# Moving the products of old states between the transposes of their own head, in an mLSTM layer streamed through TensorE

## The chip, the cores and the metric

The kernel runs on one core of one Trainium2 chip. The metric is the device time of one execution in microseconds (us); the median of the runs of one kernel is compared with the median of another.

## What is computed

The reference is one inference step of a two-layer decoder trunk, with the same weights for a prompt group (1 sequence of 256 tokens) and a sample group (8 sequences of 8 new tokens with a state from earlier steps), all in float32. Layer 0 mixes tokens by a chunked spatial gate, layer 1 by an mLSTM with 8 heads; each is followed by a gated MLP with a causal width-3 convolution. The change touches only the mLSTM of layer 1. Cut to what matters, one head's chunk of that layer computes:

```python
sc  = einsum('td,sd->ts', q, k) * w_intra               # scores inside the chunk
num = w_inter * einsum('td,de->te', q, C) + einsum('ts,se->te', sc, v)
den = w_inter * einsum('td,d->t', q, n) + sum(sc)
h   = num / max(abs(den), exp(-m_t))                    # then normed, gated by o, times w_out
C_new = decay * C + einsum('sd,se->de', k * g, v)       # the new state, an output
n_new = decay * n + sum(k * g)
```

`q`, `k` (128 wide) and `v`, `o` (256 wide) of each head come out of one product of the normed input with `b_w_in`. For the sample group `C` and `n` are inputs, one 128 x 256 matrix and one vector for each of 8 sequences and 8 heads; the prompt group starts from zero states, so for it the first term of `num` falls away. The term of the old states, `w_inter * (q C)`, and the new states `C_new` are the two places that the change moves.

## The kernel before, in words

**Blocks.** The 320 token columns (256 of the prompt, 64 of the samples) are kept transposed in SBUF. Weights are streamed once, in blocks of 128 output columns and up to 8 x 128 input rows. A block's raw float32 weights (512 KB) come by a DMA on SyncE's queue, four blocks ahead (`prefetch`, `AHEAD`), are split into a high part `wh` on ScalarE (L173) and a low part `wl` on VectorE (L174), one block ahead, and each 128 x 128 piece is multiplied three times: `wh` with the high and the low part of the input, `wl` with the high part. In the mLSTM layer a block's eight `wl` products stand last (`low_last`). A block is 24 matmuls of 128 x 320 into a PSUM buffer `pm`.

**Order.** TensorE's instructions keep the order in which the program writes them (`pin` in `mm` and `tr`, L69 and L72). The other engines' order is made by the scheduler from the program's order, data and the marks `issue_after`. PSUM is divided in two pools: `psm` with 3 buffers (blocks) and `psa` with 5 (everything else).

**The loop over heads.** `layer_b` computes the gates and the first blocks of head 0 in `gates`, then runs one iteration for each head `h`, in which blocks of head `h` alternate with what is left of head `h - 1`. Iteration `h` issues, in this order:

- `rows_in(h)` (L839): the row of decays of this head, broadcast to 128 partitions by a DMA; two blocks for `q` and `k`, each with its epilogue `qk_epi`
- `inter(h - 1)` (L947 to L955): the products of the old states. 16 matmuls `num<-C,Qz`, 32 columns of `Qz` against one sequence's state `C` (128 x 258, `n` and a padding column included), two per 32-row strip of one PSUM tile. `Qz` holds the scaled sample queries of the head, spread so that each sequence meets its own state, and is written by VectorE in `scores` (L870); for head 0 from the PSUM tile `pMb`, for the others from the row of `rows_in`
- `numer(h - 1)`: `num<-vh,Ps` (two, added to the same tile) and `num` from `vh`, `vl`, `Ph`, `Pl`, the products with `v`
- a `v` block; `stats(h - 1)`; `state_prompt(h - 1)` (`pCp`); `state_sample(h - 1, 0)`; another `v` block
- `state_sample(h - 1, 1)`, `scores(h)` (`psc`, then `w`, `dec` L868, `Qz` L870, `Pf`, `Ph`, `Pl`, `Ps`), an `o` block, `state_sample(h - 1, 2)`
- `state_in(h)` (L944): four DMAs of 258 KB, two sequences' states each, into 8 buffers `C0`; the trace calls the tile `C`
- another `o` block; `finish(h - 1)`: six transposes `phn<-ident,hn` of the normed output
- `state_sample(h - 1, 3)`: as for each pair `i`, two matmuls `pcs<-vb,kgz` or `pcs<-vh,kgz`, two VectorE updates `C<-C,dec,pcs` in place (L1032), and a DMA `out_Cs<-C` (L1033)
- `k_nat(h)`: three transposes `pk<-ident,qs` of the keys, from which ScalarE and VectorE make `kgs` (L919, L920), `kgh` and `kgl`
- `v_nat(h)`: six transposes `pv<-ident,vTb` of the values into two PSUM tiles, from which ScalarE and VectorE make `vh` (L892) and `vl` (L895)

Head 0 has no part of a head before it: in its iteration only `scores`, `k_nat` and `v_nat` stand, behind the blocks in `gates`. Its states are loaded one by one in `gates`. Head 7's iteration is written apart (`last`): `state_in(7)` stands behind its second `v` block, and `finish(6)` and the pairs 2 and 3 come earlier. Between blocks, `early` issues blocks of the output projection over the first eight pieces of the result (`pm<-yhb,wh`). Behind the loop the tail computes two pieces of that projection (`begin(0)`, `begin(1)`, four and two rows deep), then `inter(7)`, `numer(7)` and the rest of head 7.

Of the kernel before, what the change touches and what calls it, by code (L numbers as in the profile page):

```python
# [25 lines left out]
NH = 8  # L26
# [26 lines left out]
class Net:  # L53
# [622 lines left out]
    def layer_b(self):  # L676
        nc, tc, I, O = self.nc, self.tc, self.I, self.O
# [4 lines left out]
        with ExitStack() as ctx:  # L682
# [18 lines left out]
            def pairs(x):  # L701

                return x.rearrange("p (j e) -> p j e", e=16)
# [127 lines left out]
            def v_epi(h, j, ps):  # L831
                vT = lp.tile([P, 384], F32, tag="vT", name="vTb", bufs=2)
                nc.scalar.copy(vT[:, :T], ps[:, :T])
                nc.scalar.copy(vT[:, T:384], ps[:, TP:T])  # L834
                S[h].setdefault("vT", []).append(vT)
# [68 lines left out]
            def k_nat(h):  # L904
                s = S[h]
                ks = s["k"][0]
                pool, tag = (self.psm, "pm") if 0 < h < NH - 1 else (self.psa, "pa")
                pk = pool.tile([P, 512], F32, tag=tag, name="pk")
                for t in range(3):
                    self.tr(pk[:, t * P:(t + 1) * P], ks[:, t * P:(t + 1) * P], self.ident)  # L910
                kgh = hp.tile([P, 2, P], F32R, tag="kgh", name="kgh", bufs=1)
                kgl = hp.tile([P, 2, P], F32R, tag="kgl", name="kgl", bufs=1)
                kgs = hp.tile([P, 2, P], F32R, tag="kgs", name="kgs", bufs=1)
                kgz = hp.tile([P, NB, P], F32R, tag="kgz", name="kgz", bufs=1)
                g = colsT[:, 2, 32 + h:33 + h]
                src = pk[:, 2 * P:3 * P]

                for i, (r, o) in enumerate(((slice(0, 32), slice(32, 64)), (slice(32, 64), slice(0, 32)))):
                    nc.scalar.activation(kgs[:, i, :], src, AF.Copy, scale=g)  # L919
                    nc.vector.scalar_tensor_tensor(kgs[o, i, :], src[r], g[r], kgs[r, i, :].bitcast(F32), op0=MULT, op1=SUB)  # L920
                s["kg"] = (kgh, kgl, kgs, kgz)
                if h < NH - 1:
                    k_mask(h)
                for t in range(2):
                    g = colsT[:, t, 32 + h:33 + h]
                    src = pk[:, t * P:(t + 1) * P]
                    nc.scalar.activation(kgh[:, t, :], src, AF.Copy, scale=g)
                    nc.vector.scalar_tensor_tensor(kgl[:, t, :], src, g, kgh[:, t, :].bitcast(F32), op0=MULT, op1=SUB)
# [11 lines left out]
            def state_in(h):  # L940
                S[h].setdefault("C", [])
                for i in range(4) if h else (len(S[h]["C"]),):
                    C0 = lp.tile([P, 2, CW], F32, tag="C0", name="C0", bufs=8)
                    nc.sync.dma_start(C0, I["C0"][h, :, 2 * i:2 * i + 2, :])  # L944
                    S[h]["C"].append(C0)

            def inter(h):  # L947

                s = S[h]
                s["num2"] = self.psa.tile([P, 512], F32, tag="pa", name="num")  # L950
                for c in range(2):
                    for j in range(4):
                        b = 2 * j + c
                        z = NS + 32 * b - NS * c
                        mm(s["num2"][32 * j:32 * j + 32, :CW], Qz[:, z:z + 32], s["C"][j][:, c, :], c == 0, False, skip=True)  # L955
# [62 lines left out]
            def state_sample(h, i, later=False):  # L1018
                s = S[h]
                kgz, dec, C0 = s["kg"][3], s["P"][2], s["C"][i]  # L1020

                wide = h < NH - 2 or h == NH - 2 and i < 2
                pcs = [pool.tile([P, 512], F32, tag=tag, name="pcs") for pool, tag in
                       ((self.psa, "pa"), (self.psm, "pm") if wide else (self.psa, "pa"))]
                for u in range(2):
                    b = 2 * i + u
                    mm(pcs[u][:, :CW], kgz[:, b, :], vh[:, 2, :] if b < 4 else vb, True, True)

                def update():
                    for u in range(2):  # L1030
                        b = 2 * i + u
                        made = nc.vector.scalar_tensor_tensor(C0[:, u, :], C0[:, u, :], dec[:, b:b + 1], pcs[u][:, :CW], op0=MULT, op1=ADD)  # L1032
                    nc.sync.dma_start(O["Cs"][h, :, 2 * i:2 * i + 2, :], C0)  # L1033
                    return made

                return update if later else update()
# [8 lines left out]
            def finish(h):  # L1045
                s = S[h]
                yh = hp.tile([P, 2, T], F32R, tag="yhb", name="yhb", bufs=6)
                yl = hp.tile([P, 2, T], F32R, tag="ylb", name="ylb", bufs=6)
                for e in range(2):
                    pt = self.psa.tile([P, 512], F32, tag="pa", name="phn")  # L1050
                    for t in range(3):
                        self.tr(pt[:, t * P:(t + 1) * P], hn[:, t, e * P:(e + 1) * P], self.ident)
                    y = self.tp.tile([P, T], F32, tag="yf", name="y_b", bufs=2)
                    o = s["o"][e]
                    nc.vector.scalar_tensor_tensor(y[:, :TP], o[:, :TP], 1.0, pt[:, :TP], op0=ADD, op1=MULT)
                    nc.vector.scalar_tensor_tensor(pairs(y[:, TP:]), pairs(o[:, TP:]), 1.0, apart(pt[:, TP:384]), op0=ADD, op1=MULT)
                    g = gnh[:, 2 * h + e:2 * h + e + 1]
                    yp, h2, l2 = parity(y), halves(yh[:, e, :]), halves(yl[:, e, :])
                    nc.scalar.activation(h2, yp, AF.Copy, scale=g)
                    nc.vector.scalar_tensor_tensor(l2, yp, g, h2.bitcast(F32), op0=MULT, op1=SUB)  # L1060
                    Y[2 * h + e] = (yh[:, e, :], yl[:, e, :])
# [27 lines left out]
            def blk():  # L1089
                return self.block(KD, self.x_rhs)  # L1090
# [12 lines left out]
            for h in range(NH):  # L1103
                if h:
                    rows_in(h)
                    qk_epi(h, 0, blk())
                    early(h, 0)
                    qk_epi(h, 1, blk())
                    inter(h - 1)
                    numer(h - 1)  # L1110
                    early(h, 1)
                    ps = blk()
                    with self.behind_split():
                        stats(h - 1)
                    v_epi(h, 0, ps)
                    state_prompt(h - 1)
                    made = state_sample(h - 1, 0)
                    early(h, 2)
                    v_epi(h, 1, blk())
                last = h == NH - 1  # L1120
                if last:
                    with tc.issue_after(made.ins):
                        normed(h - 1)
                    with tc.issue_after(self.last_load.ins):
                        state_in(h)
                if h == 1:
                    o_epi(h, 0, blk())
                if h:
                    made = state_sample(h - 1, 1)
                    if not last:  # L1130
                        with tc.issue_after(made.ins):
                            normed(h - 1)
                scores(h)
                early(h, 3)
                if h > 1 and not last:
                    o_epi(h, 0, blk())
                if last:
                    finish(h - 1)
                    begin(0)
                if h:  # L1140
                    for i in (2, 3) if last else (2,):
                        state_sample(h - 1, i)
                if last:
                    begin(1)

                    self.prefetch(0, self.used + 2)
                early(h, 4)
                if h and not last:
                    with tc.issue_after(self.last_load.ins):
                        state_in(h)  # L1150
                if h and not last:
                    o_epi(h, 1, blk())
                if h and not last:
                    finish(h - 1)
                    state_sample(h - 1, 3)
                k_nat(h)
                v_nat(h)
                early(h, 5)
            nc.sync.dma_start(O["b_state"], nst)

            h = NH - 1
            begin(0)
            self.prefetch(0, self.used + 2)
            begin(1)
            inter(h)
            numer(h)
            ps = blk()

# [176 lines left out]
```

## Time and profile before

| | |
|---|---|
| median of 3 runs | 886.92 us (886.68 to 887.25) |
| profiled execution | 886.36 us, span 884.7 us |
| TensorE busy | 877.8 us, 6428 matmuls and transposes |
| VectorE busy | 672.6 us |
| ScalarE busy | 514.9 us |
| GpSimd busy | 109.0 us |
| read from HBM, written | 143.05 MB, 11.99 MB (175 GB/s) |
| granted TensorE clock | 1.00 |

A row of the timeline gives the start in us from the span's start, the time from the first start to the last end, the engine, the line, the operation, the output and input tiles and the shapes; `x6` says how many instructions in a row were drawn together, and a bracket gives the idle time before them and what ended it. SPq is SyncE's queue, on which DMAs are issued. Line numbers are those of the kernel before. The ends of matmuls are modelled and overlap the next ones; their starts don't.

### The profile page before, as it was taken

To read this page: it belongs to the slowest core of one execution; us is meant where nothing else is said; L and a number is where in the kernel's file an instruction comes from. 1 tells how busy PE (TensorE), PEld (TensorE's weight loads), DVE (VectorE), ACT (ScalarE), POOL (GpSimd) and SP (SyncE) were. 2 spreads that over 40 slices of the span, in tenths; PEclk is the share of its full clock that TensorE was granted. 3 is DMA by queue.
4 is the path that set the end of the run, shared out by engine and by line. 5 is a ranking of instruction groups with operands and counts; after the bars stand their busy time and mean duration, and the time that the engine had idled before them with its cause. 6 is when DMAs were issued, how large, how long until landed. Compare 5 with 4: busy or idle time off the path is not lost.

```text
span 884.7 us, 17033 instructions
## 1 busy us (share of the span) xinstructions
PE 877.8 (99%) x6428; PEld 862.7 (98%) x6428; DVE 672.6 (76%) x1290; ACT 514.9 (58%) x929; POOL 109.0 (12%) x287
## 2 busy tenths in 40 slices
PE   9999999999999999999999999999999999999997
PEld 8889999999999999999999999999999999999997
DVE  6866986678878864558999888878998888786443
ACT  7658554455555544447877776656766555554342
POOL 3200000010000000012532212203002000000000
PEclk9999999999999999999999999999999999999999
DMA  8654347645455555564756767665674544555551
GB/s 274 221 187 143 123 150 195 208 145 168 154 159 166 163 161 158 170 202 144 229 165 203 249 213 232 186 212 168 189 227 154 164 159 163 168 158 166 154 152 60
DMA packets 55238, 156.15 MB, mean 177 GB/s; under 512 B 7492, under 2 KB 13132, under 8 KB 55156
## 3 DMA queue, kind: packets, MB, share of 16 engines
q1 hardware_dynamic: 55156, 155.06, 55.9%
q8 instruction: 51, 0.84, 0.4%
q14 instruction: 31, 0.25, 0.1%
HBM read 143.05 MB, written 11.99 MB: 175 GB/s over the span
## 4 chain that ended last, share of the span: by engine, by line
PE 94%; DVE 3%; ACT 1%; issue 1%; POOL 0%; ACTq 0%; DVEq 0%; POOLq 0%
PE pm L69 80%; PE pv_a L69 6%; PE num L69 2%; PE pmix L69 1%; DVE wl L174 1%; PE pcs L69 1%; PE phn L72 1%; PE pCp L69 1%; DVE bcv L815 1%; PE pv L72 1%; PE psc L69 1%; PE pc L69 0%; PE pw L69 0%; PE pk L72 0%; ACT wh L173 0%
## 5 line engine op out<-in xcount | busy, mean ns | idle before, releaser
L173 ACT CAST wh<-raw 128x1024 fp32r<-128x1024 f32 (+4 forms) x254 | 255.6, 1007 | 219.1 <-PE pm L69 150.2
L174 DVE TENSOR_TENSOR wl<-raw,wh 128x1024 fp32r<-128x1024 f32 (+4 forms) x254 | 298.0, 1175 | 111.8 <-ACT wh L173 109.2
L69 PE MATMUL pm<-xh,wh 128*128 128x320 f32 x1216 | 356.5, 301 | 0.0
L69 PE MATMUL pm<-xl,wh 128*128 128x320 f32 x1216 | 354.4, 299 | 0.0
L69 PE MATMUL pm<-xh,wl 128*128 128x320 f32 x1216 | 308.9, 299 | 0.1
L69 PEld LDWEIGHTS pm<-xh,wh 128*128 128x128 f32 x1216 | 229.9, 189 | 0.4 <-ACT vTb L834 0.2
L69 PEld LDWEIGHTS pm<-xl,wh 128*128 128x128 f32 x1216 | 229.8, 189 | 0.2
L69 PEld LDWEIGHTS pm<-xh,wl 128*128 128x128 f32 x1216 | 211.9, 189 | 0.3 <-DVE wl L174 0.3
L69 PE MATMUL pm<-yh_f,wh 128*128 128x320 f32 x352 | 105.2, 299 | 0.0
L69 PE MATMUL pm<-yl_f,wh 128*128 128x320 f32 x352 | 105.2, 299 | 0.0
L69 PE MATMUL pm<-yh_f,wl 128*128 128x320 f32 x352 | 105.2, 299 | 0.0
L69 PEld LDWEIGHTS pm<-yh_f,wh 128*128 128x128 f32 x352 | 66.5, 189 | 0.0
L69 PEld LDWEIGHTS pm<-yl_f,wh 128*128 128x128 f32 x352 | 66.5, 189 | 0.0
L69 PEld LDWEIGHTS pm<-yh_f,wl 128*128 128x128 f32 x352 | 66.5, 189 | 0.0
L571 DVE SCALAR_TENSOR_TENSOR fcv<-fpad,vecs,fcv 128x336 f32<-128x336 f32 x88 | 49.5, 565 | 2.1 <-ACT fcv L569 0.7
L573 ACT ACTIVATE fgl<-fcv 128x256 f32<-128x256 f32 x44 | 18.3, 415 | 37.3 <-DVE fcv L571 37.3
L69 PE MATMUL pm<-yh_a,wh 128*128 128x320 f32 x128 | 38.4, 300 | 0.0
L69 PE MATMUL pm<-yl_a,wh 128*128 128x320 f32 x128 | 38.3, 299 | 0.0
L69 PE MATMUL pm<-yh_a,wl 128*128 128x320 f32 x128 | 38.3, 299 | 0.0
L69 PE MATMUL pm<-yhb,wh 128*128 128x320 f32 x128 | 35.9, 304 | 0.0
L69 PE MATMUL pm<-ylb,wh 128*128 128x320 f32 x128 | 35.4, 300 | 0.0
L339 DVE TENSOR_TENSOR xT<-pm,xT 128x320 f32<-128x320 f32 x39 | 19.1, 489 | 19.3 <-PE pm L69 19.3
(277 smaller groups left out, 1265.1 us busy)
## 6 DMA issues: line engine op xcount, KB each, us to landing
raw<-in_f_up SPq DMA_DIRECT2D x88, 512.0 KB, 3.3
raw<-in_b_win SPq DMA_DIRECT2D x48, 512.0 KB, 3.9
raw<-in_f_dn SPq DMA_DIRECT2D x32, 448.0 KB, 3.4
C<-in_C SPq DMA_DIRECT2D x32, 258.0 KB, 5.5
out_Cs<-C SPq DMA_DIRECT2D x32, 258.0 KB, 4.4
raw<-in_a_win SPq DMA_DIRECT2D x16, 512.0 KB, 3.3
raw<-in_a_wo SPq DMA_DIRECT2D x16, 512.0 KB, 4.4
raw<-in_f_dn SPq DMA_DIRECT2D x16, 512.0 KB, 3.5
```

Of the source, the lines that this page charges most:

```text
L69: self.pin(self.nc.tensor.matmul(out, lhsT, rhs, start=start, stop=stop, skip_group_check=skip))
L72: self.pin(self.nc.tensor.transpose(out, in_, ident))
L173: self.last_split = self.hold(nc.scalar.copy(wh[:, :kn, :], raw[:, :kn, :]))
L174: self.last_low = nc.vector.tensor_tensor(wl[:, :kn, :], raw[:, :kn, :], wh[:, :kn, :].bitcast(F32), op=SUB)
L339: self.nc.vector.tensor_tensor(x, ps[:, :T], x, op=ADD)
L571: nc.vector.scalar_tensor_tensor(cv, pd[:, i:i + NC], self.vec(w + i * KF), cv, op0=MULT, op1=ADD)
L573: nc.scalar.activation(gl[:, :TP], cv[:, :TP], AF.Gelu_apprx_tanh)
L815: nc.vector.scalar_tensor_tensor(cv, pd[:, i:i + NC], self.vec(w + 16 * i), cv, op0=MULT, op1=ADD)
```

## The change

- `inter(h)` goes from iteration `h + 1`, ahead of `numer(h)`, to iteration `h`, between `k_nat(h)` and `v_nat(h)`; for head 7 it goes from the tail to the end of the loop's last iteration. The PSUM tile that it begins is then taken in iteration `h`, ahead of the two of `v_nat`.
- `state_in(h)` of heads 1 to 6 goes from behind the first `o` block and the pair 2 to behind the second `v` block; an `o` block, the pairs 1 and 2 and the scores, and in heads 5 and 6 a block of the output projection too, now come between its issue and its old place.
- `state_sample(h - 1, 3)` goes ahead of `finish(h - 1)` for heads 1 to 6.

Nothing is added or taken out: both programs have the same 5549 instructions on TensorE.

```diff
                     early(h, 0)
                     qk_epi(h, 1, blk())
-                    inter(h - 1)
                     numer(h - 1)
                     early(h, 1)
                     ps = blk()
...
                     early(h, 2)
                     v_epi(h, 1, blk())
+                    if h < NH - 1:
+                        with tc.issue_after(self.last_load.ins):
+                            state_in(h)
                 last = h == NH - 1
...
                 early(h, 4)
                 if h and not last:
-                    with tc.issue_after(self.last_load.ins):
-                        state_in(h)
-                if h and not last:
                     o_epi(h, 1, blk())
                 if h and not last:
+                    state_sample(h - 1, 3)
                     finish(h - 1)
-                    state_sample(h - 1, 3)
                 k_nat(h)
+                inter(h)
                 v_nat(h)
                 early(h, 5)
...
             self.prefetch(0, self.used + 2)
             begin(1)
-            inter(h)
             numer(h)
             ps = blk()
```

## The prediction

> **What bounds the kernel now.** I read the page first (busy shares and the chain that ended last), then TensorE's waits, then TensorE's timeline around the moved step in every head, and VectorE's timeline at the places where TensorE would newly depend on it.
>
> ```profile
> span 884.7 us, 17033 instructions
> PE 877.8 (99%) x6428; PEld 862.7 (98%) x6428; DVE 672.6 (76%) x1290; ACT 514.9 (58%) x929; POOL 109.0 (12%) x287
> ...
> PE 94%; DVE 3%; ACT 1%; issue 1%; POOL 0%; ACTq 0%; DVEq 0%; POOLq 0%
> ```
>
> TensorE is busy for 99% of the span and is 94% of the chain. Its waits view has two groups:
>
> ```profile
> PE pw L69 <- PEq L1325: 0.8, 1, 0.8
> PE pcs L69 <- DVE C L1032: 0.4, 1, 0.4
> ```
>
> The columns are the sum, the count and the longest: 0.8 us before its first matmul and 0.4 us in head 1. So whatever lengthens TensorE's own sequence, or makes it wait where it doesn't wait now, goes straight into the time. There is hardly any waiting later on in which it could be paid back. Matmul rows overlap, because their ends are modelled, so below I use the distance between starts, not the durations. The timeline of TensorE around the moved step, end of one head and start of the next:
>
> ```profile
> 521.92 0.82 PE L72 MATMUL phn<-ident,hn 128*128 128x128 f32 x6
> 522.49 0.49 PE L69 MATMUL pcs<-vb,kgz 128*128 128x258 f32 x2
> 522.82 0.49 PE L72 MATMUL pk<-ident,qs 128*128 128x128 f32 x3
> 523.14 0.82 PE L72 MATMUL pv<-ident,vTb 128*128 128x128 f32 x6
> 523.72 0.38 PE L69 MATMUL pm<-yhb,wh 128*128 128x320 f32 x1
> ...
> 535.76 1.25 PE L69 MATMUL pm<-xh,wl 128*128 128x320 f32 x8
> 536.94 1.08 PE L69 MATMUL num<-C,Qz 128*32 128x258 f32 x16
> 537.95 0.50 PE L69 MATMUL num<-vh,Ps 128*128 128x258 f32 x2
> 538.29 0.29 PE L69 MATMUL num<-vh,Ph 128*128 128x258 f32 x1
> ```
>
> The moved step is the row of 16 (L69 from `inter`, the products of the old states `C` with `Qz`, 32 columns wide). The eight `wl` matmuls, of about 0.30 us each, start (1.25 - 0.30) / 7 = 0.136 us apart, so the eighth should hand over at 535.76 + 8 x 0.136 = 536.85. The step starts at 536.94: 0.09 us go in the switch to the 32-column form. It takes 1.01 us to the next start, and the two `Ps` products then take 0.34 instead of 2 x 0.12: 0.10 us more go in the switch back. I allow another 0.09 for a drain at its own end, like the one at its entry (estimate), so that all switching is about 0.28 us per head.
>
> **The moved products, steady heads.** Between the transposes the step keeps its 16 instructions, and the two switches stay: `pk` and `pv` before and after it are 128 columns wide, as the blocks are. What differs is the neighbour before it. The entry costs 0.09 us after a block matmul that streams 320 columns in 0.136 us; a transpose streams 128 of them (0.054 us by that rate) within its step of 0.11 (three `pk` from 522.82 to 523.14), so half of its step is drained already. I estimate a saving of 0.05 us per head, and 7 x 0.05 = **-0.35 us** for heads 1 to 7. Ends: all switching gone, 8 x 0.28 = -2.3 us; a dearer exit into transposes as large as today's entry, 7 x 0.09 = +0.6. I take the value near the drain because nothing in the rows makes the 32-column form cheaper beside a transpose.
>
> The Trainium skill (TensorEngine Tiling (Array Packing), Tiling Modes) says that a change of tiling mode drains TensorE; by it the number of drains is the same as before, the saving is zero and the sum below would be 0.35 us higher. The row of 0.09 us at 536.94 agrees that the change costs something.
>
> **The last pair's update ahead of the transposes of `hn`.** Six `phn`, two `pcs` take 0.90 us (521.92 to 522.82), which is 6 x 0.109 + 2 x 0.123: going from transposes to full-width matmuls and back costs nothing today. Swapping them saves nothing; I count 0. The second `pv` buffer now waits for the pair's update on DVE, but about 2.7 us of TensorE work (phn, pk, the moved step, half of pv) lies between, against 0.5 + 0.9 us of DVE work queued for it.
>
> **States loaded two blocks sooner.** Four DMA issues per head move up on SP's queue, past one weight load at most, `out_Cp` and one `out_Cs`.
>
> ```profile
> 513.74 1.93 SPq L944 DMA_DIRECT2D C<-in_C  x4
> ...
> 607.90 1.84 SPq L944 DMA_DIRECT2D C<-in_C  x4
> ...
> C<-in_C SPq DMA_DIRECT2D x32, 258.0 KB, 5.5
> ```
>
> Even at today's issue time (done at 515.7, 5.5 us to land) the states would be there at 521.2, before `pk` at 522.82, and they are issued some microseconds earlier than that. The weight load pushed behind them is wanted four blocks later (13 us). I count 0 for heads 1 to 6. Head 7's loads don't move; its states are issued from 607.90 and wanted at 624.
>
> **Head 0.** This is the term that decides. Here the products used to come after two blocks of head 1, and now they come right behind `pk` of head 0, which itself stands right behind `scores(0)`, where `Qz` is made. TensorE's timeline and then VectorE's:
>
> ```profile
> 416.98 0.49 PE L72 MATMUL pk<-ident,qs 128*128 128x128 f32 x3
> 417.31 0.82 PE L72 MATMUL pv<-ident,vTb 128*128 128x128 f32 x6
> 417.88 0.38 PE L69 MATMUL pm<-xh,wh 128*128 128x320 f32 x1
> ...
> 424.58 1.08 PE L69 MATMUL num<-C,Qz 128*32 128x258 f32 x16
> 425.80 0.47 PE L69 MATMUL num<-vh,Ps 128*128 128x258 f32 x2
> ```
>
> ```profile
> 416.60 2.36 DVE L174 TENSOR_TENSOR wl<-raw,wh 128x1024 fp32r<-128x1024 f32 x2
> 418.88 0.48 DVE L1040 TENSOR_TENSOR o_b<-pm,rb 128x320 f32<-128x320 f32 x1
> ...
> 419.65 1.21 DVE L174 TENSOR_TENSOR wl<-raw,wh 128x1024 fp32r<-128x1024 f32 x1
> ...
> 420.99 0.17 DVE L868 COPY dec<-pMb 128x8 f32<-128x8 f32 x1
> 421.07 0.21 DVE L870 SCALAR_TENSOR_TENSOR Qz<-qs,pMb 128x64 f32<-128x64 f32 x1
> ```
>
> `Qz` of head 0 is written at 421.28: VectorE has three weight splits, an `o_b` and small work queued ahead of it, without a gap. Today TensorE spends that time on `pv` and two blocks and reads `Qz` at 424.58, so nobody notices. In the changed program VectorE's queue up to this `Qz` is the same, instruction for instruction, and nothing in it waits for TensorE work that comes after `pk`; so `Qz` still ends at 421.28. TensorE is in order and comes to the step at 417.31 + 0.04 = 417.35. A result of VectorE reaches TensorE about 0.15 us later (estimate: of the two updates in the row at 439.07 below, 0.86 us together, the first ends at about 439.07 + 0.43 = 439.50 or a little later, and the matmul that waits for it starts at 439.69). It starts at 421.43: a wait of **+4.1 us**. Queued behind it are `pv`, both blocks of head 1 and all that follows; ScalarE and VectorE then wait for `pv`. The cover that is gone is the two blocks (6.5 us). Ends: 3.8 and 4.4 us, if the splits ahead shift by a quarter of one.
>
> **Given back in head 1.** VectorE catches up meanwhile, so the small waits that its backlog causes shrink. At 425.80 TensorE starts 1.22 us after the step's start instead of 1.01, and:
>
> ```profile
> 439.07 0.86 DVE L1032 SCALAR_TENSOR_TENSOR C<-C,dec,pcs 128x258 f32<-128x258 f32 x2
> ```
>
> ```profile
> 434.81 0.40 PE L69 MATMUL pm<-xh,wh 128*128 128x320 f32 x1
> 435.05 0.30 PE L69 MATMUL pm<-xl,wh 128*128 128x320 f32 x1
> ...
> 438.76 0.55 PE L69 MATMUL psc<-qs 128*128 128x128 f32 x4
> 439.69 0.48 PE L69 MATMUL pcs<-vb,kgz 128*128 128x258 f32 x2 [0.37 <-DVE C L1032]
> ```
>
> About 0.2 at 425.80, 0.2 around 434.8 (0.14 late, then a step of 0.24 for 0.136), and of the 0.57 us before 439.69 perhaps 0.2, since the update that it waits for can't start before its own product is there. **-0.6 us**, ends 0 and -1.0.
>
> **Head 7.** Here only two short pieces (1.6 us) lie between `pv` and its use, not two blocks.
>
> ```profile
> 624.28 0.49 PE L72 MATMUL pk<-ident,qs 128*128 128x128 f32 x3
> ...
> 626.99 1.08 PE L69 MATMUL num<-C,Qz 128*32 128x258 f32 x16
> 628.00 0.50 PE L69 MATMUL num<-vh,Ps 128*128 128x258 f32 x2
> ...
> 629.33 0.39 PE L69 MATMUL num<-vl,Ph 128*128 128x258 f32 x1
> ```
>
> ```profile
> 627.27 1.23 DVE L174 TENSOR_TENSOR wl<-raw,wh 128x1024 fp32r<-128x1024 f32 x1
> ...
> 628.80 0.47 DVE L895 SCALAR_TENSOR_TENSOR vl<-pv,rc,vh 128x256 fp32r<-128x256 f32 x1
> ```
>
> The `vl` that ends at 629.27 already holds the product at 629.33. The moved step pushes `pv` back by 1.1 us while TensorE reaches `numer` at the same time as now. If `vl` keeps its distance to `pv`, it ends 1.1 us later and TensorE waits for it: **+1.1 us**. Ends: 0 (the queue of VectorE makes room) and +2.3 (a second split of 1.2 us stands ahead of it; the changed queue does have both splits before the last `vl`).
>
> **The sum.** 4.1 - 0.6 - 0.35 + 1.1 = +4.25 us. The profiled execution took 886.36 us (span 884.7 and 1.66 around it): 890.6. The median of the three runs shown is 0.56 higher, 886.92; carried to it, **891.2 us**, the predicted time.
>
> **Rivals.**
> - *The clock falls in the wait.* TensorE would stand still for 4.05 us.
>
> ```profile
> 879.14 0.33 PE L69 MATMUL pb<-ident,rcf 128*128 128x64 f32 x2
> ...
> 883.00:884.70 1.70, 0.00 (x0) 0.00 (x0) 0.00 (x0) 0.00 (x0) 0.00 (x0) 0.91 0.08 28
> ```
>
>   The last number but two is the granted clock. 0.91 over 1.70 us is half speed for 0.31 us, so it fell at 884.4, 4.9 us after the last matmul ended at 879.47. A wait of 4.05 us is shorter, which speaks against it; that the one fall shown needn't be the earliest possible speaks for it. If the low clock then stays 4.9 us as well, 2.45 us are lost: 893.6. Chance 0.12. The Trainium skill (TensorE: Matmul & The Clock Gate, Part 1) has a free-running window of 3413 ns, an idle one halving the clock and a busy one restoring it; by it a 4.05 us pause holds a whole window in about one run of five and costs some 1.7 us, 892.9. The 4.9 us of the row agrees with it.
> - *The switches vanish between transposes.* All 0.28 us per head are saved: 4.1 - 0.6 - 2.3 + 1.1 = +2.3, 889.2. For it: the step stands among float32 work of the same kind. Against: the width still changes twice. Chance 0.08. Together with no loss in head 7 it gives 888.1, within 0.2%: 0.04.
> - *Faster.* One mechanism: `Qz` of head 0 comes early, so that the wait is under the 2.3 us that the switches could save, which decides at `Qz` by about 419.5. If it stood ahead of the splits on VectorE, some 0.4 us after `pMb` lands (about 417.2), the wait would be 0.4 us and the time 886.92 + 0.4 - 0.6 - 2.3 + 1.1 = 885.5. The order of the changed queue speaks against it. Chance 0.02.
> - *The loads aren't in time*, so that heads 1 to 6 wait for states: the rows above leave several microseconds; I give it no case of its own.
>
> **How the numbers follow.** Forecast case 0.74 (889.8 to 892.4 by the bounds of head 7 and head 0), clock 0.12, switches 0.08, both savings 0.04, faster 0.02. The range of 889.0 to 893.0 takes in the forecast, the switch case and the lower part of the clock case, leaving out about 0.14. A measurement of this kernel can tell about 0.2% (1.8 us) from no change: slower 0.94, within 0.04, faster 0.02.
>
> **What would show it.** In the changed profile: TensorE idle for about 4 us before the first `num<-C,Qz`, ended by DVE `Qz` L870, between 417 and 422; no wait for `C` loads; the step at about 1.0 us in heads 1 to 6, with an entry near 0.04; no wait at 434.8 + shift; a wait of about 1 us at `num<-vl,Ph` of head 7; granted clock 1.00 throughout. I am wrong if `Qz` is written sooner in head 0, if the clock drops behind the wait, or if the distance from `pk` to `pv` around the step is clearly under 1.1 us.

## The result, and the profile after

The changed kernel takes **895.08 us** (median of 5, 894.02 to 896.54) against 886.99 us (median of 5, 886.68 to 887.27): a ratio of **1.0093**, 95% interval 1.0082 to 1.0105. It is slower by 8.1 us where 4.25 were forecast (891.2, range 889.0 to 893.0), so the direction was right and the size was not. The profiled execution took 895.23 us, 8.87 more than the one before. Both profiles record 6428 matmuls and transposes on TensorE; the 5549 given with the change is the count of neither.

First the page of the kernel after (span, busy shares, chain), then TensorE's waits (sum, count, longest; the wait at the start is left out here).

```profile
span 893.5 us, 17030 instructions
PE 881.0 (99%) x6428; PEld 864.6 (97%) x6428; DVE 676.1 (76%) x1290; ACT 513.5 (57%) x929; POOL 114.2 (13%) x287
...
PE 86%; DVE 7%; ACT 2%; DMA 2%; issue 2%; SPq 0%; POOL 0%; DVEq 0%; ACTq 0%
```

```profile
PE num L69 <- issue: 3.9, 1, 3.9
...
PE num L69 <- DVE vl L895: 0.7, 1, 0.7
PE psc L69 <- DVE C L1032: 0.5, 1, 0.5
...
PE num L69 <- DVE vh L895: 0.4, 1, 0.4
PE pm L69 <- DVE ylb L1060: 0.2, 1, 0.2
```

The share of busy time still reads 99%, but the chain has gone from 94% to 86% TensorE, and VectorE has 7% of it. Where two wait groups stood, five new ones of the mLSTM layer stand. They hold 5.7 us; the rest isn't a wait.

**Head 0.** TensorE's timeline of the kernel after, then VectorE's:

```profile
417.45 0.49 PE L72 MATMUL pk<-ident,qs 128*128 128x128 f32 x3
421.85 1.95 PE L69 MATMUL num<-C,Qz 128*32 128x258 f32 x16 [3.92 <-issue]
423.73 1.54 PE L72 MATMUL pv<-ident,vTb 128*128 128x128 f32 x6
...
425.60 0.47 PE L69 MATMUL pm<-xh,wh 128*128 128x320 f32 x1
...
427.58 0.30 PE L69 MATMUL pm<-xh,wh 128*128 128x320 f32 x1
```

```profile
420.12 1.22 DVE L174 TENSOR_TENSOR wl<-raw,wh 128x1024 fp32r<-128x1024 f32 x1
...
421.54 0.21 DVE L870 SCALAR_TENSOR_TENSOR Qz<-qs,pMb 128x64 f32<-128x64 f32 x1
```

The three `pk` end their steps at 417.45 + 3 x 0.108 = 417.77, and the step starts at 421.85: a pause of 4.08 us. The view names no releaser ("issue"). The step starts 0.1 us after `Qz` is written at 421.75, and it starts at once in a run below that leaves out this write. Behind it the same instructions take longer: the step 1.88 us to its next start instead of 1.01, a block's matmul 0.47 instead of 0.30. In this trace the granted clock changes at 420.58, at 427.41 and, in the idle end of the kernel, at 891.62: 6.83 and 464.21 us apart, 2 and 136 times 3.4133. The windows view laid on that grid says why (columns: window, its length, busy time of TensorE, of its weight loads, of VectorE, ScalarE, GpSimd, then the granted clock, DMA share and GB/s):

```profile
417.17:420.58 3.41, 0.77 (x6) 0.51 (x4) 3.41 (x5) 0.87 (x3) 2.04 (x7) 1.00 0.38 129
420.58:424.00 3.42, 2.15 (x18) 0.95 (x18) 3.31 (x9) 2.54 (x8) 2.23 (x5) 0.50 0.93 301
424.00:427.41 3.41, 3.41 (x15) 3.41 (x15) 2.81 (x7) 2.82 (x9) 2.01 (x4) 0.50 0.45 179
427.41:430.80 3.39, 3.39 (x26) 3.39 (x26) 1.14 (x4) 1.98 (x4) 1.18 (x3) 1.00 0.00 0
```

The clock fell to half in the pause and came back 6.83 us later, after a window that was wholly busy. From 421.85 to the first full-speed start at 427.44 went 5.59 us; at the full clock the same instructions take 1.01 for the step, 0.63 for the six `pv`, and 0.22 + 8 x 0.136 to the tenth matmul of the block: 2.95. The half clock costs **2.64 us** in this execution. Other differences lie between executions too, and what makes them is open: of this kernel, one with a mean granted clock of 0.998 took 895.08 us and one with 0.995 took 895.00.

**A steady head**, TensorE around the step between the transposes:

```profile
530.06 0.49 PE L72 MATMUL pk<-ident,qs 128*128 128x128 f32 x3
530.48 1.08 PE L69 MATMUL num<-C,Qz 128*32 128x258 f32 x16
531.49 0.87 PE L72 MATMUL pv<-ident,vTb 128*128 128x128 f32 x6
532.12 0.38 PE L69 MATMUL pm<-yhb,wh 128*128 128x320 f32 x1
```

The step takes 1.01 us as before and its entry 530.48 - 530.06 - 3 x 0.109 = 0.09 more than a transpose, as before too. The exit is cheaper: the six `pv` take 0.63 to the next start, 0.05 more than the 0.58 that they took behind `pk` (523.14 to 523.72 before), where two `Ps` products lost 0.10. About 0.045 us a head is saved.

**Heads 3 and 4.** New waits, of `psc` (scores) in heads 3 and 4 and of an early block in head 4. TensorE after and before at `psc` of head 4:

```profile
521.52 0.36 PE L69 MATMUL psc<-qh,kh 128*128 128x256 f32 x1 [0.51 <-DVE C L1032]
```

```profile
514.35 0.28 PE L69 MATMUL psc<-qh,kh 128*128 128x256 f32 x1
```

`psc` takes a PSUM tile from which VectorE's update of the first pair has to read first. That update after, and before:

```profile
520.90 0.47 DVE L1032 SCALAR_TENSOR_TENSOR C<-C,Mb,pcs 128x258 f32<-128x258 f32 x1
```

```profile
512.18 0.47 DVE L1032 SCALAR_TENSOR_TENSOR C<-C,Mb,pcs 128x258 f32<-128x258 f32 x1
```

Before, it ended 1.7 us ahead of `psc`; after, 0.15 us ahead of it, and `psc` had waited for it. VectorE has fallen behind TensorE by over 2 us. The same groups hold the reason, `ylb` on VectorE and `kgz` on GpSimd, after and before:

```profile
532.77 1.80 DVE L1060 SCALAR_TENSOR_TENSOR ylb<-y_b,gnh,yhb 128x320 fp32r<-128x320 f32 x2
```

```profile
532.82 1.40 POOL L937 TENSOR_TENSOR kgz<-kgs,mk 128x512 fp32r<-128x512 f32 x1 [10.23 <-DVE kgs L920]
```

```profile
523.91 1.19 DVE L1060 SCALAR_TENSOR_TENSOR ylb<-y_b,gnh,yhb 128x320 fp32r<-128x320 f32 x2
```

```profile
526.02 2.04 POOL L937 TENSOR_TENSOR kgz<-kgs,mk 128x512 fp32r<-128x512 f32 x2 [12.16 <-DVE kgs L920]
```

Before, `kgz` came 0.9 us after both `ylb`. After, the pair's two updates stand ahead of `y_b` and `ylb` in VectorE's queue, `kgs` has passed `ylb`, GpSimd starts on `kgs` at 532.82, and the second `ylb` takes 1.33 us (to 534.57, 0.35 us behind the end of `kgz`) instead of 0.55. From one `Qz` to the next VectorE then needs 27.0 us in head 3, where it took 26.2 before.

**Head 7**, the two waits of `numer` and VectorE's instructions that end them:

```profile
636.20 0.51 PE L69 MATMUL num<-vh,Ps 128*128 128x258 f32 x2 [0.42 <-DVE vh L895]
...
638.24 0.39 PE L69 MATMUL num<-vl,Ph 128*128 128x258 f32 x1 [0.68 <-DVE vl L895]
```

```profile
635.66 0.49 DVE L895 SCALAR_TENSOR_TENSOR vh<-pv,rc,vh 64x256 fp32r<-64x256 f32 x1
...
637.70 0.48 DVE L895 SCALAR_TENSOR_TENSOR vl<-pv,rc,vh 128x256 fp32r<-128x256 f32 x1
```

The sum for the profiled execution: pause 4.08, half clock 2.64, `psc` of heads 3 and 4 and the early block 0.22 + 0.81 + 0.49 = 1.52, head 7 1.29 (0.58 for `vh` and 0.95 for `vl`, less 0.24 that stood there before), the small waits given back up to head 1 -0.80, seven switches -0.32, and 0.47 in start-up waits of layer 0 that have nothing to do with the change (in the profiles of all kernels here they are 0 to 0.9 us longer than in the kernel before's): 8.88 of 8.87 us. The -0.80 is what is left of the 5.83 us by which the way from `pMb` of head 0 to `pCp` of head 1 grew, when pause, half clock and two switches are taken off.

### The profile page after: what moved, and what is told of

Read it like the earlier page. It is cut to its first block, busy times and chain, and to the rows that moved or that the text cites. A ratio compares the mean times of both kernels' runs of the same rounds, so it can differ in the third digit from the quotient of the medians.

```text
span 893.5 us, 17030 instructions
## 1 busy us (share of the span) xinstructions
PE 881.0 (99%) x6428; PEld 864.6 (97%) x6428; DVE 676.1 (76%) x1290; ACT 513.5 (57%) x929; POOL 114.2 (13%) x287
## 4 chain that ended last, share of the span: by engine, by line
PE 86%; DVE 7%; ACT 2%; DMA 2%; issue 2%; SPq 0%; POOL 0%; DVEq 0%; ACTq 0%
PE pm L69 75%; PE pv_a L69 6%; DVE wl L174 1%; DVE bcv L815 1%; PE num L69 1%; DMA Mb<-rows 1%; DVE C L1032 1%; PE pmix L69 1%; PE pcs L69 1%; ACT wh L173 1%; DMA raw<-in_a_wv 0%; DMA raw<-in_b_win 0%; PE pv L72 0%; PE psc L69 0%; PE pCp L69 0%
```

## The experiments

Theory A is this sum. Rival B: the half clock costs nothing by itself. Rival C: VectorE is late because the moved products push `pv` back, or as an after-effect of the pause, not through the swap of the pair. Each was run in five or more executions; the kernel before gave 886.89 to 887.02 us beside them.

**Head 0's products back at their old place.**

```diff
                 k_nat(h)
-                inter(h)
+                if h:
+                    inter(h)
...
+                    if h == 1:
+                        inter(0)
                     numer(h - 1)
```

> The changed kernel with head 0's products of old states back in head 1 ahead of numer; the rest of the change stays. Theory A (the 8.1 us are a wait of 4.1 us for Qz of head 0, 2.6 us of matmuls at half clock behind it, about 1.5 us because VectorE falls behind in heads 2 to 4, 1.2 us in head 7, less 0.7 us given back in head 1 and 0.35 us of switches): 895.1 - 4.1 - 2.6 + 0.7 = 889.1 us, up to 890 if VectorE falls behind further without the pause in head 0; no wait for Qz, granted clock 1.00 in the layer. Rival B (the half clock costs nothing by itself): 895.1 - 4.1 + 0.7 = 891.7 us. Rival C (VectorE falls behind only as an after-effect of the pause): 887.6 us.

Measured: 889.25 us (888.76 to 890.57), ratio 1.0029 (1.0018 to 1.0039). As A has it. Granted clock 1.00 in the layer, no wait for `Qz`; the waits of `psc` in head 4 and of `numer` in head 7 are as in the changed kernel, so they aren't after-effects of the pause. Head 0 is worth 5.8 us of the 8.1.

**Head 0's products alone moved, in the kernel before.**

```diff
-                    inter(h - 1)
+                    if h > 1:
+                        inter(h - 1)
                     numer(h - 1)
...
                 k_nat(h)
+                if not h:
+                    inter(h)
                 v_nat(h)
```

> The kernel before with head 0's products alone moved between its transposes. Theory A: 887.0 + 4.1 + 2.6 - 0.7 = 893.0 us, half clock for some 3 to 7 us behind the wait. Rival B (the half clock costs nothing by itself): 890.4 us.

Measured: 891.37 us (891.11 to 891.77), ratio 1.0050 (1.0037 to 1.0062): between the two. The step starts behind the same wait and is as slow:

```profile
421.39 1.82 PE L69 MATMUL num<-C,Qz 128*32 128x258 f32 x16 [3.92 <-issue]
```

The windows view shows that here the half clock lasted one window, not two:

```profile
418.17:421.59 3.42, 0.20 (x4) 0.19 (x8) 3.40 (x8) 1.76 (x5) 1.84 (x5) 1.00 0.67 196
421.59:425.00 3.41, 3.41 (x24) 2.40 (x17) 2.79 (x7) 2.27 (x7) 2.42 (x4) 0.50 0.93 354
425.00:428.40 3.40, 3.40 (x26) 3.40 (x26) 2.10 (x6) 3.35 (x9) 1.41 (x4) 1.00 0.08 28
```

The grid of 3.41 us lies elsewhere in each execution. Here the pause fills one window, and the window behind it is wholly busy and ends the half clock; in the changed kernel's profile the pause straddled two, and the second (2.15 us busy) was too idle to end it.

**The same with the pause filled**: 24 products that nobody uses, into the tile that the step starts afresh.

```diff
                 s["num2"] = self.psa.tile([P, 512], F32, tag="pa", name="num")
+                if not h:
+                    for i in range(24):
+                        mm(s["num2"][:, :T], self.onesr, weave(self.xh[:, i % KD, :]), True, True)
```

> As the run with head 0's products alone moved, but with 24 products of a constant with the input, 320 columns each (3.3 us of work that nobody uses, written into the PSUM tile that the products of old states then start afresh), in the place of the wait. Theory A: TensorE stays at granted clock 1.00, the products still start when Qz comes, 887.0 + 4.1 - 0.7 = 890.4 us, 2.6 us less than without the filling. Rival B (the half clock costs nothing by itself): the same time as without the filling. A third possibility: the filling delays VectorE or ScalarE, then more than without it.

Measured: 890.10 us (889.71 to 890.99), ratio 1.0036 (1.0024 to 1.0049), granted clock 1.00 throughout. The step still starts with `Qz`:

```profile
421.88 1.08 PE L69 MATMUL num<-C,Qz 128*32 128x258 f32 x16 [0.66 <-issue]
```

It lasts 1.08 us, not 1.82 as without the filling. More work in the same place is 1.3 us cheaper, which speaks against B: the half clock is a cost of its own, here of one window. Counted in the profiles from the start of `pMb` to that of the last matmul, the filled kernel takes 465.70 us and the unfilled one 467.38: 1.68 us, half of a window of 3.41.

**Half of the filling**, 12 products instead of 24.

> As the run with 24 products of a constant in the place of the wait, with 12 of them: TensorE is busy to about 419.4 us and idle for 2.4 us instead of 4 or 0.7. If the clock falls whenever most of a 3.4 us stretch is idle, as the stretches of 6 and 23% busy time did that fell, it may still fall in some executions; if it takes a busy share under about 30%, it doesn't: 890.1 us as with 24. If any pause over some 2 us halves it: 891.4 us as with none.

Measured: 890.10 us (889.86 to 890.45), ratio 1.0035 (1.0021 to 1.0048), as with 24. TensorE stood still for 2.3 us, spread over two windows, and the clock stayed:

```profile
417.69:421.11 3.42, 2.27 (x16) 2.00 (x16) 3.42 (x5) 0.88 (x3) 2.04 (x7) 1.00 0.50 132
421.11:424.52 3.41, 2.28 (x27) 1.77 (x28) 3.30 (x9) 2.42 (x8) 2.36 (x5) 1.00 0.84 269
```

The grid of this trace is reckoned back from the fall of the clock in the kernel's idle end, at 888.73. The ends of the kernels show the rule without any wait: TensorE's last matmul stands somewhere inside a stretch. First this kernel, then the one with `ylb` held ahead of `kgs` (below):

```profile
881.90:885.31 3.41, 1.68 (x16) 1.54 (x14) 2.25 (x5) 1.28 (x3) 0.97 (x2) 1.00 0.43 157
885.31:888.73 3.42, 0.00 (x0) 0.00 (x0) 0.00 (x0) 0.00 (x0) 0.00 (x0) 1.00 0.59 226
```

```profile
887.87:891.29 3.42, 1.23 (x12) 1.09 (x10) 2.03 (x4) 1.27 (x2) 0.53 (x1) 1.00 0.56 210
891.29:894.28 2.99, 0.00 (x0) 0.00 (x0) 0.00 (x0) 0.00 (x0) 0.00 (x0) 0.50 0.52 198
```

A stretch with 1.68 us of work kept the clock, and it fell a whole stretch later, 5.2 us after the last matmul's end at 883.57; behind a stretch with 1.23 us it fell at once, 2.2 us after the last matmul's end at 889.10.

**The write of `Qz` left out for head 0**, products of head 0 moved as above.

```diff
+                if h:
-                nc.vector.scalar_tensor_tensor(Qd, seg(q[:, TP:T]), 0.5, ...
+                  nc.vector.scalar_tensor_tensor(Qd, seg(q[:, TP:T]), 0.5, ...
```

> As the run with head 0's products alone moved, but VectorE's instruction that writes Qz of head 0 is left out (Qz keeps its zeros, so the old states' term of head 0 is missing from the output). Theory A (all that the moved products of head 0 cost hangs on the wait for Qz, the half clock included): no wait, no half clock, 887.0 less a few tenths, 886.7 us, against 891.4 with the wait. Rival (the place itself costs, by pv and all behind it 1 us later): 887.5 us or more.

Measured: 888.71 us (887.85 to 890.41), ratio 1.0024 (1.0015 to 1.0032). A expected 886.7; that is missed. The step starts at once, but behind the one wait stands another:

```profile
421.75 0.44 PE L72 MATMUL pv<-ident,vTb 128*128 128x128 f32 x2 [2.15 <-DVE dec L868]
```

The step's PSUM tile takes the last of the five `psa` buffers, so the second `pv` tile has to take that of `pMb`, which VectorE reads for `dec` just ahead of `Qz`, behind the same splits. Even a `Qz` that came at once would have left 2.1 us, as long as `dec` stays where it is. The executions lie in two groups, 887.9 to 888.8 with a granted clock of 0.999 over the span and 890.1 to 890.4 with 0.997; the profiled one is of the second:

```profile
418.77:422.18 3.41, 1.26 (x16) 0.85 (x9) 3.27 (x7) 1.89 (x6) 1.82 (x5) 1.00 0.79 208
422.18:425.59 3.41, 3.41 (x15) 3.41 (x14) 3.24 (x8) 2.79 (x9) 1.71 (x3) 0.50 0.90 357
```

So one kernel with a pause of 2.15 us falls to half clock in some executions (by their times and clocks 4 of 11) and not in others, and one window of it costs some 1.7 us.

**The last pair's update alone ahead of the transposes of `hn`.**

```diff
+                    state_sample(h - 1, 3)
                     finish(h - 1)
-                    state_sample(h - 1, 3)
```

> The kernel before with the last pair's update ahead of the transposes of hn, and nothing else of the change. Theory A (the swap lets kgs pass ylb in VectorE's queue, so that GpSimd's kgz runs beside ylb): ylb stretched here too, 0.8 us a head, 887.0 + 1.0 to 1.8 = 888.0 to 888.8 us. Rival C (the moved products make VectorE late, not the swap): 887.0 us.

Measured: 889.38 us (888.42 to 889.53), ratio 1.0026 (1.0016 to 1.0036). C falls as an explanation of this part: nothing is moved here but the pair, and it costs 2.5 us (the kernel before gave 886.89 beside it), more than A said. VectorE, GpSimd and TensorE in head 4:

```profile
525.59 1.43 DVE L1060 SCALAR_TENSOR_TENSOR ylb<-y_b,gnh,yhb 128x320 fp32r<-128x320 f32 x1
```

```profile
525.63 1.04 POOL L937 TENSOR_TENSOR kgz<-kgs,mk 128x512 fp32r<-128x512 f32 x1 [10.24 <-DVE kgs L920]
```

```profile
527.08 0.40 PE L69 MATMUL pm<-ylb,wh 128*128 128x320 f32 x1 [0.75 <-DVE ylb L1060]
```

`ylb` begins with `kgz` and ends 0.35 us after it, while `kgz` takes the 1.04 us that it takes alone. What TensorE waits for is other than in the changed kernel: the early blocks of heads 4, 5 and 6 come right behind `pv` and need `ylb` 1 us sooner.

**`kgz` held behind `ylb`, in the changed kernel.**

```diff
+                if 0 < h < NH - 1:
+                    late = hp.tile([P, 8], F32, tag="late", name="late", bufs=1)
+                    self.pin(nc.gpsimd.tensor_copy(late, Y['last'][:, :8].bitcast(F32)))
                 for i in (0, 4):
-                    nc.gpsimd.tensor_tensor(kgz[:, i:i + 4, :], ...
+                    self.pin(nc.gpsimd.tensor_tensor(kgz[:, i:i + 4, :], ...
...
                     Y[2 * h + e] = (yh[:, e, :], yl[:, e, :])
+                    Y['last'] = yl[:, e, :]
```

> The changed kernel with one small GpSimd copy (128 x 8) from the second ylb ahead of each kgz pair in heads 1 to 6, so that GpSimd starts kgz only when ylb is done; VectorE's and ScalarE's queues keep their order, instruction for instruction. Theory A (the second ylb is stretched from 0.55 to 1.33 us by GpSimd's kgz beside it, which makes VectorE need 27 us a head where TensorE needs 26.2, until TensorE waits): ylb at 0.55 us, the waits for VectorE at psc of heads 3 and 4 and at the early block of head 4 gone, 895.1 - 1.4 = 893.7 us. Rival C (VectorE is late because pv comes 1.1 us later, or through its changed order): those waits stay, 895.1 us.

Measured: 894.63 us (893.18 to 894.92), ratio 1.0086 (1.0072 to 1.0100).

```profile
531.17 1.01 DVE L1063 SCALAR_TENSOR_TENSOR ylb<-y_b,gnh,yhb 128x320 fp32r<-128x320 f32 x2
```

```profile
532.39 2.04 POOL L940 TENSOR_TENSOR kgz<-kgs,mk 128x512 fp32r<-128x512 f32 x2
```

All `ylb` are back at 0.55 us with VectorE's and ScalarE's queues in the same order, so `kgz` is what stretches them. The waits of heads 3 and 4 shrink from 1.52 to 0.46 us in the profiles. They don't vanish, and the second `kgz` now runs beside VectorE's next split, which takes 1.62 us at 533.89 instead of 1.22; whether that is the rest isn't shown. The median follows by 0.45 us only, and the two kernels' executions overlap: the time of the one effect can't be read from these medians. In this profile the pause left one stretch wholly idle, and the next, 3.03 us busy, ended the half clock:

```profile
418.26:421.68 3.42, 0.00 (x0) 0.00 (x0) 3.42 (x7) 1.39 (x4) 1.90 (x4) 1.00 0.55 177
421.68:425.09 3.41, 3.03 (x22) 1.84 (x23) 3.26 (x9) 2.08 (x6) 2.43 (x6) 0.50 0.90 323
```

**`ylb` held ahead of `kgs` on VectorE, in the changed kernel.**

```diff
-                    nc.vector.scalar_tensor_tensor(l2, yp, g, ...)
+                    self.pin(nc.vector.scalar_tensor_tensor(l2, yp, g, ...))
...
-                    nc.vector.scalar_tensor_tensor(kgs[o, i, :], ...)
+                    self.pin(nc.vector.scalar_tensor_tensor(kgs[o, i, :], ...))
```

> The changed kernel with VectorE's ylb instructions held ahead of the next kgs ones in its queue, as the program writes them, so that GpSimd's kgz starts behind them. Theory A with this cause (the second ylb takes 1.33 us beside GpSimd's kgz instead of 0.55, 0.8 us per head, until scores and an early block wait): ylb back to 0.55 us, the waits of psc and pm for VectorE in heads 3 and 4 gone, 895.1 - 1.5 = 893.6 us. Rival C (VectorE is late because pv comes 1.1 us later): those waits stay, 895.1 us.

Measured: 894.81 us (894.54 to 896.02), ratio 1.0089 (1.0075 to 1.0103). It decides nothing: `ylb` is at 0.55 us, but the waits of `psc` grew to 1.4 us, and the fixed order makes VectorE stand still elsewhere; that this costs as much as was gained is argued, not shown.

```profile
511.08 0.34 DVE L920 SCALAR_TENSOR_TENSOR kgs<-pk,cols,kgs 32x128 fp32r<-32x128 f32 x1 [2.05 <-ACT kgs L919]
```

The pause of head 0 is in this profile too: a stretch with 1.05 us of work fell, and one with 1.86 us didn't end the half clock.

```profile
416.84:420.25 3.41, 1.05 (x9) 0.78 (x7) 3.38 (x6) 0.98 (x2) 2.04 (x7) 1.00 0.40 139
420.25:423.67 3.42, 1.86 (x16) 0.68 (x16) 3.00 (x9) 2.55 (x9) 1.26 (x4) 0.50 0.86 271
```

**The swap undone in the changed kernel.**

```diff
-                    state_sample(h - 1, 3)
                     finish(h - 1)
+                    state_sample(h - 1, 3)
```

> The changed kernel with the last pair's update behind the transposes of hn again. Theory A (of the 8.1 us the swap costs 1.4 to 2 by way of VectorE's ylb beside GpSimd's kgz): ylb at 0.55 us, no waits for ylb, 893.1 to 893.7 us; head 0's wait and head 7's waits stay. Rival (VectorE is late without the swap too, by the moved products): 895.1 us.

Measured: 892.91 us (892.38 to 894.00), ratio 1.0069 (1.0056 to 1.0082): 2.2 us less than the changed kernel, a little more than A has. In the profiles the waits of heads 3 and 4 go from 1.52 to 0.30 us; the other 1.0 between the profiles is the half clock, of one window in this one and two in the other, which the swap has no part in. The 0.30 that stay, at `psc` of heads 3 and 4, are an effect that C names. `psc` is on time both where head 0's products alone are moved and where those of heads 1 to 6 are moved without the swap (below), so it seems to take both; how isn't shown.

**Heads 0 and 7 at their old places**, from the changed kernel.

```diff
+                    if h == 1:
+                        inter(0)
                     numer(h - 1)
...
-                inter(h)
+                if 0 < h < NH - 1:
+                    inter(h)
...
             begin(1)
+            inter(h)
             numer(h)
```

> The changed kernel with the products of old states of heads 0 and 7 back at their old places. Theory A (head 7 loses 1.2 us, because pv comes 1.1 us later and numer waits for vh and vl): 889.25 - 1.2 = 888.05 us, waits at numer of head 7 as in the kernel before. Rival (those waits only stand in for others behind them): 889.25 us.

Measured: 888.64 us (887.32 to 889.09), ratio 1.0016 (1.0008 to 1.0025): 0.6 us under the kernel with head 0 alone put back. The waits at `numer` of head 7 are gone, and the piece from `pCp` of head 6 to that of head 7 loses 0.10 us against the kernel before, where it lost 1.36 with head 0 alone put back: 1.26 us, as A says. The medians show half of it; the executions lie in two groups (887.3 to 887.8, the profiled one among them, and 888.5 to 889.1), and what divides these stays open.

**Only heads 1 to 6 and the earlier loads**: as the last one, with the swap undone too.

> As the run with heads 0 and 7 at their old places, with the last pair's update behind the transposes of hn too: what is left of the change is the moved products of heads 1 to 6 and the earlier loads of states. Theory A (the swap is behind VectorE's lateness): ylb at 0.55 us, no waits for VectorE at psc, 888.05 - 1.4 = 886.65 us, 0.3 us under the kernel before by six cheaper switches of 0.045 us. Rival C (the moved products make VectorE late, not the swap): 888.05 us.

Measured: 886.57 us (886.19 to 887.03, 11 executions), ratio 0.9997 (0.9988 to 1.0005). A's 886.65 holds, C's 888.05 doesn't. The profile keeps only the old wait of `pcs` in head 1 in this layer, every `ylb` is at 0.55 us, and TensorE gains 0.04 to 0.07 us in each of heads 1 to 6. It is the best version seen, 0.3 us under the kernel before, which the interval doesn't tell from nothing.

**The states alone loaded sooner.**

```diff
                     v_epi(h, 1, blk())
+                    if h < NH - 1:
+                        with tc.issue_after(self.last_load.ins):
+                            state_in(h)
...
                 early(h, 4)
-                if h and not last:
-                    with tc.issue_after(self.last_load.ins):
-                        state_in(h)
```

> The kernel before with the states of heads 1 to 6 loaded sooner, and nothing else of the change. Both theories: no engine's queue but SP's changes, no wait for a load before or after, 886.9 us within 0.2. A difference over 0.2% would mean that the loads are in the way of the weights.

Measured: 886.93 us (886.63 to 888.87), ratio 1.0002 (0.9993 to 1.0010). No difference.

## Why the prediction was wrong

- **Head 0's wait** (+4.1): right, 4.08 us, with the releaser named. Its cover was gone as said. That a second wait, for `pMb`'s buffer, stood behind it wasn't seen. The "faster" rival, 885.5, needed an early `dec` as well as an early `Qz`: without the write of `Qz`, but with `dec` where it is, the kernel takes 888.7.
- **The clock** failed. The prediction put the chance of half clock at 0.12, because "a wait of 4.05 us is shorter" than the 4.9 us after which the one fall shown came. All five profiled executions with the unfilled wait fell. The fall isn't a fixed delay after the last matmul (2.2 and 5.2 us at the ends of two kernels) but follows the work in a stretch of 3.41 us: it came behind the pause's stretches of 0.00, 0.07, 0.20, 0.77, 1.05 and 1.26 us busy, and not behind those of 2.27, 2.28 and 2.76 us or the 1.68 us at a kernel's end. Busy is the profile's count, in which the ends of matmuls are modelled. A pause of 4.1 us leaves at least one stretch with no more than 3.41 - 2.04 = 1.37 us of work, close to the largest that fell; one of 2.15 us leaves so little in some executions only. The price was 1.3 us (medians, filled against unfilled; 1.68 in the profiles) to 2.64 us (the changed kernel's profile), since behind it not every stretch brings the clock back: 1.86 and 2.15 us busy didn't do, 3.03 and 3.41 did. The Trainium skill (TensorE: Matmul & The Clock Gate, Part 1) has the free-running window of 3413 ns right; it says one idle window halves the clock, and here a window 37% busy did so too, where one 49% busy didn't. The one-in-five chance that the prediction drew from that sentence came from asking for a wholly idle window.
- **The swap at 0** failed. The step "Swapping them saves nothing; I count 0" looked at TensorE and the PSUM buffer. It didn't ask what VectorE's own order becomes: the updates go ahead of `y_b`, `kgs` ahead of `ylb`, and `kgz` runs beside `ylb`. It costs 1.2 us of waits in the changed kernel's profile (1.52 with it, 0.30 with the swap undone) and 2.5 us where it stands alone. The Trainium skill (SBUF — State Buffer, SBUF: two separate sides) says that a VectorE instruction with two SBUF inputs and a GpSimd instruction that reads SBUF exclude each other for the whole of the instruction; the trace agrees in that `ylb` takes 1.43 us around a `kgz` of 1.04 and ends 0.35 us behind it. Which of the two goes first it doesn't show: that `ylb` had started 0.04 us ahead of `kgz` and is still the one that is held. The prediction didn't weigh it for this pair.
- **Head 7** (+1.1): right, 1.29 in the profile, though by two waits, for `vh` and for `vl`.
- **Given back** (-0.6): right, -0.80. **States sooner** (0): right.
- **Switches** (-0.35): right in size (-0.32) by luck, and wrong in place. The entry, where the saving was expected, stayed at 0.09 us; the exit into transposes is the cheaper one. With the rule of the Trainium skill (TensorEngine Tiling (Array Packing), Tiling Modes) that a change of mode drains TensorE, the prediction weighed a saving of zero; 0.045 us a head is small enough that no median here tells the two apart.

With the two failed terms at their profiled sizes (2.64 and 1.52 in place of 0), the prediction's own sum is 895.3 us.

## What to carry to other kernels

When a reorder makes a busy TensorE wait, price the clock as well as the wait: lay stretches of 3.41 us over the pause, and if one can come out less than about half busy (37% fell, 49% and more didn't), add half of TensorE's busy time up to the end of the next full stretch. Matmuls that nobody uses, 1.6 or 3.3 us of them in a pause of 4.1, saved that here in all ten executions. The shorter filling is not safe by these figures: it leaves 2.29 us of pause, and one of 2.15 us fell in 4 of 11 executions of another kernel. And when a step is moved, read the new order of every engine that has no pinned order, for pairs that now run side by side: here one swap on TensorE changed who stands beside whom on VectorE and GpSimd, and that cost more than anything the move could win.

## What the runs showed of the hardware that was not expected

- The clock's stretches are 3.41 us long and lie elsewhere in each execution, so the same pause can cost one stretch, two or none: 890.1 to 890.4 us against 887.9 to 888.8 in one kernel.
- Filling a pause with 1.6 us of useless matmuls made a kernel 1.3 us faster.
- A 128x320 instruction of VectorE took 1.33 to 1.43 us instead of 0.55 beside GpSimd's 128x512 product, on other tiles.
